# A decoder trunk on one core: the seventh product of a token-major step is issued inside the next channel-major step, and the first such step of each layer comes later

## The chip, the cores and the metric

The kernel runs on one core of a Trainium2 chip. The core has five engines with queues of their own: TensorE (PE in the profile; its weight loads are PEld), VectorE (DVE), ScalarE (ACT), GpSimd (POOL) and SyncE (SP), which issues the loads of weights. The metric is device time in microseconds of one execution. The kernel before has three runs: 2107.92, 2093.62 and 2107.99 us, median 2107.92.

## The reference

Two layers of a hybrid decoder on 256 tokens of width 2048, in float32. The core of a layer:

```python
h = rms_norm(x, norm1_g[l])
z = h @ w_in[l]                       # 2048 x 5120: q, k, v, gu, gv
mix = concatenate([attn(q, k, v), gmlp(gelu(gu), gelu(gv))])
x = x + mix @ w_out[l]                # 2048 x 2048
h2 = rms_norm(x, norm2_g[l])
x = x + square(relu(h2 @ w_up[l])) @ w_down[l]   # 2048 x 8192, 8192 x 2048
```

After both layers comes a last `rms_norm`. Nearly all of the work is the four weight products, and the two of the MLP (`w_up`, `w_down`) are about two thirds of it. The change is in the MLP.

## The kernel before, in words

**Numbers.** TensorE multiplies fp32r. To keep float32's accuracy each operand is split: `hi` is the value rounded to fp32r by a copy on ScalarE (L152, L170), `lo` the rest, by a subtraction on VectorE (L162, L175). A product is three matmuls: hi by hi, lo by hi, hi by lo. Activations are split in the same way; they lie in `hs` (the normalised input of a projection), `half` (1024 channels of an MLP's inner value) and `shared` (sums of pieces of `half`).

**Layout.** `x` stands transposed: 16 chunks of 128 channels by 256 tokens. A **channel-major step** (`transposed`, L352 to L385) takes a 512 x 256 piece of weights, with the weights stationary and 256 tokens moving: 2 column halves of 4 products, 24 matmuls of 128 x 256 into a bank `acc` (L380, L382, L384). A **token-major step** (`fast`, L387 to L413) has the activations stationary and 256 columns of weights moving. It computes a part of `w_down`'s first 512 columns with seven products of half-size blocks in place of eight, in the manner of Strassen and Winograd: seven products of 2 chunks of 3 matmuls, 42 matmuls (L408, L410, L411), which all accumulate in four banks `aux` that stay taken from a layer's first such step to its last. It needs four pieces: `Top`, `Bottom`, and two `Sums` of them that VectorE makes in place (L202 to L206). Of the activations, three of the seven products use `half` and four use `shared`, sums of blocks of `half` that VectorE makes (L729 to L732) and that are split in four parts (L611, L612).

**Order.** The MLP of a layer runs in nine rounds, `e` = 0 to 8. A round issues `w_up` for 1024 inner channels (16 steps; not in round 9), and `w_down` for the 1024 of the round before (not in round 1): 12 channel-major steps for columns 512 to 2047, and 2 token-major steps for columns 0 to 511. The token-major steps are put among the `w_up` steps (in round 9 among the `w_down` steps): behind the 4th and 8th of 16, and in round 9 behind the 3rd and 6th of 12. This list is written out (`steps`), and the program issues it step by step: ScalarE's `hi` and VectorE's `lo` are issued up to four steps ahead, loads as buffers come free (`load_more`). Other work (`later(delay, cost, fn)`) waits in a queue that is looked at once behind each step and spends a budget of 1.2 there; `soon` is for the same without a budget. The sums come by this queue behind a round's last `w_up` step, one part a step; `sums_ready()` issues what is still missing when a token-major step begins.

**A layer's end.** Behind the last token-major step `combine` (L741 to L753) reads the four banks and makes the four result blocks with seven additions on VectorE. Two `turn_back` (L755 to L761) transpose two blocks each on TensorE (four 128 x 128 transposes, L760), and `update` adds the result to `x` chunks 0, 1 and 2, 3 (L471, `x<-x,aux`). In layer 0 an update is followed by `hs` for the next layer (ScalarE L269, VectorE L273), a square (ScalarE L282) and the sum of squares (VectorE L286, `nacc`). In layer 1 the squares go to the last norm: a matmul with ones (L297), a square root (ScalarE L320), the spread of the factor (L305), the products with `x` (L877), and the stores.

In the program each engine executes its own instructions in the order in which they are issued.

Of the kernel before, what the change touches and what calls it, by code (L numbers as in the profile page):

```python
# [83 lines left out]
def trunk(ctx: ExitStack, tc: tile.TileContext, layout, xT, consts, gains, w, b_sp, w_sp, out):  # L84
# [37 lines left out]
    def acc_bank():  # L122
        return pacc.tile([P, 512], F32, name="acc", tag="acc")

    def aux_bank():
        return paux.tile([P, 512], F32, name="aux", tag="aux")
# [58 lines left out]
    class Bottom(Sub):  # L185


        left, right, frees = Top.left, Top.right, 0
# [23 lines left out]
    cols = cp.tile([P, (2 * DEPTH + 1) * KC + 2 * DEPTH * NH], F32, name="cols")  # L212
# [14 lines left out]
    def later(delay, cost, fn):  # L227

        queue.append((now[0] + delay, cost, fn))
# [107 lines left out]


    steps = []
    summed, sum_parts = [True], [None]  # L340

    def sums_ready():
        run_until(lambda: summed[0])

    def collect(fn, *args, **kw):
        n = len(steps)
        fn(*args, **kw)
        part = steps[n:]
        del steps[n:]
        return part  # L350

    def transposed(name, l, row0, nk, col0, ncols, moving, after, between=None, apart=False):  # L352

        order = [(c, k) for c in range(0, ncols, 256) for k in range(0, nk, 4)]
        if between:  # L360
            h = nk // 8
            order[h:2 * h], order[2 * h:3 * h] = order[2 * h:3 * h], order[h:2 * h]
        accs = {}
        for n, (c, k0) in enumerate(order):
            if between and n == nk // 4:
                mark(between)
            wt = Sub(name, l, row0 + k0 * P, col0 + c, 4, 256)

            def mm(wt=wt, k0=k0, c=c):
                two = apart and c == ncols - 256  # L370
                if k0 == 0:
                    accs[c] = [acc_bank(), acc_bank()] if two else acc_bank()
                ps = accs[c]
                for cb in range(2):
                    o = ps[cb][:, 0:S] if two else ps[:, cb * S:(cb + 1) * S]
                    for k in range(4):
                        xs = moving(k0 + k)
                        hi = wt.hi[:, k, cb * P:(cb + 1) * P]
                        last = k0 + k == nk - 1
                        pe.matmul(o, lhsT=hi, rhs=xs[:, 0, :], start=(k0 + k == 0 and (two or cb == 0)), stop=False,  # L380
                                  skip_group_check=True)
                        pe.matmul(o, lhsT=wt.lo[:, k, cb * P:(cb + 1) * P], rhs=xs[:, 0, :], start=False, stop=False,  # L382
                                  skip_group_check=True)
                        pe.matmul(o, lhsT=hi, rhs=xs[:, 1, :], start=False, stop=last, skip_group_check=True)  # L384
            steps.append((wt, mm, (lambda c=c: after(c, accs[c])) if k0 + 4 == nk else None))  # L385

    def fast(name, l, row0, col0, tiles, banks, first, last, done):  # L387

        for p in range(2):
            top, bottom = (cls(name, l, row0 + (4 * h + 2 * p) * P, col0, 2, 512) for h, cls in enumerate((Top, Bottom)))  # L390
            upper, lower = Sums(top, bottom, False), Sums(top, bottom, True)

            def mm(p=p, top=top, bottom=bottom, upper=upper, lower=lower):
                if first and p == 0:
                    banks.extend(aux_bank() for _ in range(4))
                half = tiles[0][0]
                sums_ready()
                extra = sum_parts[0]
                left, right = slice(0, 256), slice(256, 512)
                for n, (a, lower_rows, tt, b, cols) in enumerate((  # L400
                        (half, 0, 0, top, left), (half, 1, 0, bottom, left), (extra, 1, 0, bottom, right),
                        (extra, 1, 1, upper, left), (extra, 0, 1, upper, right),
                        (extra, 0, 0, lower, right), (half, 1, 1, lower, left))):
                    o = banks[n // 2][:, n % 2 * 256:n % 2 * 256 + 256]
                    for k in range(2):
                        xh, xl = (a[:, 4 * lower_rows + 2 * p + k, i, tt * P:(tt + 1) * P] for i in range(2))
                        hi, lo = b.hi[:, k, cols], b.lo[:, k, cols]
                        pe.matmul(o, lhsT=xh, rhs=hi, start=(first and p == 0 and k == 0 and n % 2 == 0), stop=False,  # L408
                                  skip_group_check=True)
                        pe.matmul(o, lhsT=xh, rhs=lo, start=False, stop=False, skip_group_check=True)  # L410
                        pe.matmul(o, lhsT=xl, rhs=hi, start=False, stop=(last and p == 1 and k == 1),  # L411
                                  skip_group_check=True)
            steps.append(((top, bottom, upper, lower), mm, done if p and last else None))  # L413

    def natural(name, l, col0, ncols, after):
# [20 lines left out]
    def mark(fn):  # L436

        steps.append((None, fn, None))
# [4 lines left out]
    def from_tiles(tiles, n):  # L443
        return lambda k: tiles[k // n][0][:, k % n, :, :]
# [21 lines left out]
    def update(norm, c, ps, final, last):  # L466

        alone = last and final and c == KC - 2
        for j in range(2) if alone else [slice(0, 2)]:
            xj = x[:, c + j, :] if alone else x[:, c:c + 2, :]  # L470
            vec.tensor_tensor(xj, xj, ps[j][:, 0:S] if alone else pair(ps)[:, j, :], op=OP.add)  # L471
        if final:
            if not last:
                norm.chunks(c)
            norm.square(c, alone)
            if last:
                norm.gain(c)

    def layer(l, n1, n2, n3, last):
# [261 lines left out]
        def combine():  # L741
            p1, p2, p3, p5, p7, p6, p4 = (banks[n // 2][:, n % 2 * 256:n % 2 * 256 + 256] for n in range(7))
            b1, u, c11, c12, c21, c22 = (blocks[:, n, :] for n in range(6))
            act.activation(b1, p1, AF.Copy)
            vec.tensor_tensor(u, b1, p6, op=OP.add)
            vec.tensor_tensor(c11, b1, p2, op=OP.add)
            vec.tensor_tensor(c22, u, p7, op=OP.add)
            vec.tensor_tensor(u, u, p5, op=OP.add)
            vec.tensor_tensor(c12, u, p3, op=OP.add)
            vec.tensor_tensor(c21, c22, p4, op=OP.subtract)  # L750
            vec.tensor_tensor(c22, c22, p5, op=OP.add)
            later(1, 1.5, lambda: turn_back(0, c11, c21))
            later(1, 1.5, lambda: turn_back(2, c12, c22))  # L753

        def turn_back(c, first, second):  # L755
            ps = aux_bank()
            for j in range(2):
                for tt, src in enumerate((first, second)):
                    o = j * S + tt * P
                    pe.transpose(ps[:, o:o + P], src[:, j * P:(j + 1) * P], ident)  # L760
            later(0, 1.5, lambda: update(n3, c, ps, True, last))  # L761
# [3 lines left out]
        for e in range(9):  # L765
            up, down, quick = [], [], []
            if e < 8:
                up = collect(transposed, "w_up", l, 0, KC, e * 1024, 1024, from_hs, after_up(e))
            if e:
                down = collect(transposed, "w_down", l, (e - 1) * 1024, 8, FAST, D - FAST, from_tiles([hid[e - 1]], NH),  # L770
                               lambda c, ps, e=e: update(n3, (c + FAST) // P, ps, e == 8, last), apart=last and e == 8)
                quick = collect(fast, "w_down", l, (e - 1) * 1024, 0, [hid[e - 1]], banks, e == 1, e == 8,
                                lambda: later(1, 1.5, combine))
            rest = up or down
            n = len(quick) + 1
            for i in range(n):
                steps.extend(rest[len(rest) * i // (n + 1):len(rest) * (i + 1) // (n + 1)] if quick else rest)
                steps.extend(quick[i:i + 1])
            if quick:
                steps.extend(rest[len(rest) * n // (n + 1):])  # L780
            if up:
                steps.extend(down)
        if last:
# [11 lines left out]
    for l in range(DEPTH):  # L795
        layer(l, norms[2 * l], norms[2 * l + 1], norms[2 * l + 2], l == DEPTH - 1)
# [74 lines left out]
    n = norms[-1]  # L871
# [43 lines left out]
```

## Time and profile before

| | |
|---|---|
| runs | 2107.92, 2093.62, 2107.99 us (median 2107.92) |
| profiled execution | 2093.35 us, span 2091.5 us, mean granted clock 0.994 |
| TensorE | 2066.8 us busy, 17066 matmul records |
| VectorE | 1464.4 us busy, 1800 instructions |
| ScalarE | 1008.9 us busy, 1265 instructions |
| HBM | 390.65 MB read, 188 GB/s over the span |

How to read it: times are microseconds from the span's start. A row of a timeline gives start, length, engine, line and operation with `out<-in`, and in brackets the idle time ahead of it with what ended it; neighbouring instructions of one kind are merged (`x2`). Matmuls are pipelined: a matmul of 256 columns is shown as about 280 ns long, but the next starts some 115 ns after it, so TensorE's busy share says that it had work, not how quickly it went through it. A row of a table of stretches gives the stretch, its length, TensorE's busy time with the count of matmuls, the granted clock, the share of the DMA engines and GB/s.

### The profile page before, as it was taken

What the parts mean: (1) busy time and instruction counts of PE and PEld (TensorE: products, weight loads), DVE (VectorE), ACT (ScalarE), POOL (GpSimd) and SP (SyncE); (2) the same over time, 40 slices, a digit from 0 to 9 for tenths busy, and PEclk for the clock granted to TensorE, in tenths of its full rate; (3) what the DMA queues carried; (4) which work ended last, traced back from release to release, by engine and by line L of the source; (5) the groups of instructions that cost most, each with busy time, mean ns of one, the idle gap of its engine ahead of it and who ended that gap; (6) DMA issues with size and microseconds to landing.
All of it is one profiled execution on the core that took longest, in us unless ns stands there. A gap on an engine that the chain in (4) does not pass through costs nothing. (4 is left out here: it accounts for less than half of the span.)

```text
span 2091.5 us, 40406 instructions
## 1 busy us (share of the span) xinstructions
PE 2066.8 (99%) x17066; PEld 2028.3 (97%) x17066; DVE 1464.4 (70%) x1800; ACT 1008.9 (48%) x1265; POOL 68.7 (3%) x90
## 2 busy tenths in 40 slices
PE   9999999999999999999999999999999999999997
PEld 8998999899999999999989999998999999999997
DVE  7666766777677677776856576667676676777666
ACT  7555454444454444544645554545353444444444
POOL 0002300000000000000000050000000000000000
PEclk9999999999999999999999999999999999999998
DMA  8555555365565655656565556555565655556543
GB/s 320 175 172 177 196 183 191 134 225 190 172 218 178 226 192 169 216 182 201 189 204 172 183 172 197 185 181 173 170 207 177 216 188 178 196 178 216 191 162 111
DMA packets 112118, 395.38 MB, mean 189 GB/s; under 512 B 12352, under 2 KB 16448, under 8 KB 111936
## 3 DMA queue, kind: packets, MB, share of 16 engines
q1 hardware_dynamic: 110800, 389.86, 55.6%
q8 instruction: 133, 2.18, 0.4%
q10 hardware_dynamic: 1136, 2.94, 0.4%
q14 instruction: 49, 0.40, 0.1%
HBM read 390.65 MB, written 2.10 MB: 188 GB/s over the span
## 5 line engine op out<-in xcount | busy, mean ns | idle before, releaser
L152 ACT ACTIVATE hi<-raw 128x1024 fp32r<-128x1024 f32 (+1 forms) x773 | 783.7, 1046 | 420.8 <-PE acc L384 194.5
L162 DVE TENSOR_TENSOR lo<-raw,hi 128x1024 fp32r<-128x1024 f32 (+1 forms) x773 | 907.8, 1211 | 42.0 <-ACT hi L152 25.8
L380 PE MATMUL acc<-hs,hi 128*128 128x256 f32 x2816 | 784.3, 279 | 0.0
L384 PE MATMUL acc<-hs,hi 128*128 128x256 f32 x2816 | 781.8, 278 | 0.0
L382 PE MATMUL acc<-hs,lo 128*128 128x256 f32 x2816 | 781.8, 278 | 0.0
L380 PE MATMUL acc<-half,hi 128*128 128x256 f32 x2048 | 569.5, 278 | 0.0
L382 PE MATMUL acc<-half,lo 128*128 128x256 f32 x2048 | 569.1, 278 | 0.0
L384 PE MATMUL acc<-half,hi 128*128 128x256 f32 x2048 | 569.0, 278 | 0.0
L380 PEld LDWEIGHTS acc<-hs,hi 128*128 128x128 f32 x2816 | 532.3, 189 | 0.4 <-issue 0.2
L382 PEld LDWEIGHTS acc<-hs,lo 128*128 128x128 f32 x2816 | 528.8, 188 | 0.4 <-issue 0.2
L384 PEld LDWEIGHTS acc<-hs,hi 128*128 128x128 f32 x2816 | 528.6, 188 | 0.0
L380 PEld LDWEIGHTS acc<-half,hi 128*128 128x128 f32 x2048 | 387.6, 189 | 0.0
L382 PEld LDWEIGHTS acc<-half,lo 128*128 128x128 f32 x2048 | 384.4, 188 | 0.1
L384 PEld LDWEIGHTS acc<-half,hi 128*128 128x128 f32 x2048 | 384.4, 188 | 0.0
L611 ACT ACTIVATE half<-ar 128x512 fp32r<-128x512 f32 x72 | 45.6, 633 | 323.5 <-DVE ar L716 308.9
L471 DVE TENSOR_TENSOR x<-x,acc 128x512 f32<-128x512 f32 (+1 forms) x113 | 76.7, 680 | 174.6 <-PE acc L384 174.6
L715 DVE TENSOR_TENSOR ar<-acc,nR 128x512 f32<-128x512 f32 x64 | 44.2, 691 | 196.0 <-PE acc L384 196.0
L431 PE MATMUL acc<-hi,hs 128*128 128x512 f32 x256 | 101.4, 396 | 0.5 <-ACT hs L269 0.5
L433 PE MATMUL acc<-hi,hs 128*128 128x512 f32 x256 | 100.8, 394 | 0.0
L432 PE MATMUL acc<-lo,hs 128*128 128x512 f32 x256 | 100.1, 391 | 0.0
L612 DVE TENSOR_TENSOR half<-ar,half 128x512 fp32r<-128x512 f32 x72 | 49.8, 692 | 50.3 <-ACT half L611 50.3
L408 PE MATMUL aux<-hi,shared 128*128 128x256 f32 x256 | 73.4, 287 | 10.4 <-ACT shared L611 10.4
(127 smaller groups left out, 1548.2 us busy)
## 6 DMA issues: line engine op xcount, KB each, us to landing
raw<-in_w SPq DMA_DIRECT2D x731, 512.0 KB, 4.5
raw<-in_w SPq DMA_DIRECT2D x10, 256.0 KB, 5.3
x<-in_xT SPq DMA_DIRECT2D x7, 256.0 KB, 5.6
out<-x SPq DMA_DIRECT2D x7, 256.0 KB, 3.1
shared<-in_b_sp ACTq DMA_DIRECT2D x2, 512.0 KB, 7.0
shared<-in_w_sp ACTq DMA_DIRECT2D x2, 512.0 KB, 8.5
con<-in_consts ACTq DMA_DIRECT2D x1, 512.0 KB, 7.4
x<-in_xT ACTq DMA_DIRECT2D x1, 256.0 KB, 4.2
```

The lines of the kernel that those rows point to most:

```text
L152: act.activation(self.h[:, j * m:(j + 1) * m], self.raw[:, j * m:(j + 1) * m], AF.Copy)
L162: vec.tensor_tensor(lo[:, r], self.raw[:, r], self.h[:, r].bitcast(F32), op=OP.subtract)
L380: pe.matmul(o, lhsT=hi, rhs=xs[:, 0, :], start=(k0 + k == 0 and (two or cb == 0)), stop=False, skip_group_check=True)
L382: pe.matmul(o, lhsT=wt.lo[:, k, cb * P:(cb + 1) * P], rhs=xs[:, 0, :], start=False, stop=False, skip_group_check=True)
L384: pe.matmul(o, lhsT=hi, rhs=xs[:, 1, :], start=False, stop=last, skip_group_check=True)
L408: pe.matmul(o, lhsT=xh, rhs=hi, start=(first and p == 0 and k == 0 and n % 2 == 0), stop=False, skip_group_check=True)
L431: pe.matmul(ps, lhsT=xh, rhs=hi, start=(k0 + k == 0), stop=False)
L432: pe.matmul(ps, lhsT=xh, rhs=lo, start=False, stop=False)
L433: pe.matmul(ps, lhsT=xl, rhs=hi, start=False, stop=(k0 + k == KC - 1))
L471: vec.tensor_tensor(xj, xj, ps[j][:, 0:S] if alone else pair(ps)[:, j, :], op=OP.add)
L611: act.activation(t[:, c:c + 2, 0, :], src, AF.Copy)
L612: vec.tensor_tensor(t[:, c:c + 2, 1, :], src, t[:, c:c + 2, 0, :].bitcast(F32), op=OP.subtract)
```

## The change

It has three parts. (1) A token-major step computes six of its products; the seventh is put into a list `held`, and the next channel-major step issues it behind its own first three matmuls. (2) The places of the token-major steps are given by step: in round 2, the first that has any, behind the 8th and the 12th `w_up` step (before: 4th and 8th), in rounds 3 to 8 behind the 4th and 8th (as before), in round 9 behind the 4th and 8th `w_down` step (before: 3rd and 6th). (3) `turn_back` is put off by two steps in place of one.

```diff
+    held = []
...
                     for k in range(4):
+                        if cb == 0 and k == 1 and held:
+                            held.pop()()
                         xs = moving(k0 + k)
...
-                for n, (a, lower_rows, tt, b, cols) in enumerate((
-                        (half, 0, 0, top, left), (half, 1, 0, bottom, left), (extra, 1, 0, bottom, right),
-                        (extra, 1, 1, upper, left), (extra, 0, 1, upper, right),
-                        (extra, 0, 0, lower, right), (half, 1, 1, lower, left))):
+
+                def product(n, a, lower_rows, tt, b, cols):
                     o = banks[n // 2][:, n % 2 * 256:n % 2 * 256 + 256]
                     for k in range(2):
...
+                for n, args in enumerate((
+                        (half, 0, 0, top, left), (half, 1, 0, bottom, left), (extra, 1, 0, bottom, right),
+                        (extra, 1, 1, upper, left), (extra, 0, 1, upper, right), (extra, 0, 0, lower, right))):
+                    product(n, *args)
+                held.append(lambda: product(6, half, 1, 1, lower, left))
...
-            later(1, 1.5, lambda: turn_back(0, c11, c21))
-            later(1, 1.5, lambda: turn_back(2, c12, c22))
+            later(2, 1.5, lambda: turn_back(0, c11, c21))
+            later(2, 1.5, lambda: turn_back(2, c12, c22))
...
-            n = len(quick) + 1
-            for i in range(n):
-                steps.extend(rest[len(rest) * i // (n + 1):len(rest) * (i + 1) // (n + 1)] if quick else rest)
-                steps.extend(quick[i:i + 1])
-            if quick:
-                steps.extend(rest[len(rest) * n // (n + 1):])
+            at = (8, 12) if e == 1 else (4, 8)
+            for i, one in enumerate(rest):
+                if quick and i in at:
+                    steps.append(quick.pop(0))
+                steps.append(one)
```

TensorE, end of a token-major step in round 2 or later, before: the sixth product's last matmul (`shared`), the seventh product (`half`, its three matmuls stand twice), and the channel-major step behind it.

```order
L411 MATMUL aux<-hi,shared 128x256
L408 MATMUL aux<-hi,half 128x256
L410 MATMUL aux<-lo,half 128x256
L411 MATMUL aux<-hi,half 128x256
L408 MATMUL aux<-hi,half 128x256
L410 MATMUL aux<-lo,half 128x256
L411 MATMUL aux<-hi,half 128x256
L380 MATMUL acc<-hs,hi 128x256
L382 MATMUL acc<-hs,lo 128x256
L384 MATMUL acc<-hs,hi 128x256
```

The same place of the changed kernel, whose lines are numbered some higher:

```order
L414 MATMUL aux<-hi,shared 128x256
L383 MATMUL acc<-hs,hi 128x256
L385 MATMUL acc<-hs,lo 128x256
L387 MATMUL acc<-hs,hi 128x256
L411 MATMUL aux<-hi,half 128x256
L413 MATMUL aux<-lo,half 128x256
L414 MATMUL aux<-hi,half 128x256
L411 MATMUL aux<-hi,half 128x256
L413 MATMUL aux<-lo,half 128x256
L414 MATMUL aux<-hi,half 128x256
L383 MATMUL acc<-hs,hi 128x256
```

The seventh product's six matmuls moved behind three matmuls of the channel-major step, which goes on behind them.

ScalarE in round 2 of layer 0, before, from the last `w_up` product of round 1 (`half`, the first row): `hi` of 128 x 512 is the first token-major step's `Top`, the next three `hi` belong to it too (`Bottom` and the two `Sums`), and the four `shared` are the parts of the sums.

```order
L611 ACTIVATE half<-ar 128x2x256
L152 ACTIVATE hi<-raw 128x1024 x2
L611 ACTIVATE shared<-ar 128x2x256
L152 ACTIVATE hi<-raw 128x1024
L611 ACTIVATE shared<-ar 128x2x256
L152 ACTIVATE hi<-raw 128x1024
L611 ACTIVATE half<-ar 128x2x256
L611 ACTIVATE shared<-ar 128x2x256
L152 ACTIVATE hi<-raw 128x1024
L611 ACTIVATE shared<-ar 128x2x256
L152 ACTIVATE hi<-raw 128x1024 x2
L170 ACTIVATE hi<-raw 128x512
```

The same place in the changed kernel, from the same row:

```order
L620 ACTIVATE half<-ar 128x2x256
L152 ACTIVATE hi<-raw 128x1024 x2
L620 ACTIVATE shared<-ar 128x2x256
L152 ACTIVATE hi<-raw 128x1024
L620 ACTIVATE shared<-ar 128x2x256
L170 ACTIVATE hi<-raw 128x512
L620 ACTIVATE half<-ar 128x2x256
L620 ACTIVATE shared<-ar 128x2x256
L152 ACTIVATE hi<-raw 128x1024
L620 ACTIVATE shared<-ar 128x2x256
L152 ACTIVATE hi<-raw 128x1024 x3
L620 ACTIVATE half<-ar 128x2x256
```

Before, the first step's `Top` stood ahead of the first of these rows, and the `hi` of 128 x 512 at the end is the second token-major step's; now the one between the second and third `shared` is the first step's, and all four `shared` are issued while channel-major steps are still to come.

VectorE at the end of layer 0, before, from the last `lo` ahead of an update (names with buffer numbers): `x<-x,acc` adds a channel-major block to `x`, `x<-x,aux` a block that came by `turn_back`.

```order
L162 TENSOR_TENSOR lo_11816<-raw_11694,hi_11778 128x1024
L471 TENSOR_TENSOR x_82<-x_82,acc_11784 128x512
L273 SCALAR_TENSOR_TENSOR hs_83<-x_82,cols_80,hs_83 128x256 x2
L286 TENSOR_TENSOR nacc_11424<-nacc_11424,nsq_11849 128x512
L471 TENSOR_TENSOR x_82<-x_82,aux_11773 128x512
L273 SCALAR_TENSOR_TENSOR hs_83<-x_82,cols_80,hs_83 128x256 x2
L286 TENSOR_TENSOR nacc_11424<-nacc_11424,nsq_11857 128x512
L162 TENSOR_TENSOR lo_11862<-raw_11696,hi_11814 128x1024
L471 TENSOR_TENSOR x_82<-x_82,aux_11809 128x512
```

And in the changed kernel:

```order
L162 TENSOR_TENSOR lo_11880<-raw_11757,hi_11842 128x1024
L480 TENSOR_TENSOR x_82<-x_82,acc_11848 128x512
L273 SCALAR_TENSOR_TENSOR hs_83<-x_82,cols_80,hs_83 128x256 x2
L286 TENSOR_TENSOR nacc_11422<-nacc_11422,nsq_11913 128x512
L480 TENSOR_TENSOR x_82<-x_82,aux_11873 128x512
L273 SCALAR_TENSOR_TENSOR hs_83<-x_82,cols_80,hs_83 128x256 x2
L286 TENSOR_TENSOR nacc_11422<-nacc_11422,nsq_11930 128x512
L162 TENSOR_TENSOR lo_11935<-raw_11759,hi_11878 128x1024
L480 TENSOR_TENSOR x_82<-x_82,aux_11916 128x512
```

The rows read alike, but the `x<-x,acc` among them is before the one of step 10 of round 9's twelve, with the last block's to follow behind both `x<-x,aux`; in the changed kernel it is the last block's, and behind it stand only the two `x<-x,aux`. In layer 1 the last block's update, in two halves of 128 x 256, stood behind both `x<-x,aux` and now stands ahead of them.

## The prediction

> **What bounds the kernel now.** I read the page first, then TensorE's waits, then busy time by stretches, because a TensorE that is always busy can still run at two speeds. In the fence: the page's head and first part, and TensorE's waits (line waited for: us in all, times, longest).
>
> ```profile
> span 2091.5 us, 40406 instructions
> ...
> PE 2066.8 (99%) x17066; PEld 2028.3 (97%) x17066; DVE 1464.4 (70%) x1800; ACT 1008.9 (48%) x1265; POOL 68.7 (3%) x90
> ...
> PE aux L408 <- ACT shared L611: 10.4, 2, 5.2
> PE aux L305 <- DVE nr L331: 1.2, 1, 1.2
> PE aux L760 <- DVE ar L750: 1.1, 1, 1.1
> ```
>
> TensorE sets the time: 99% busy, and the only long waits are two of 5.2 us, one a layer, in a token-major step (L408) for the last piece of `shared`. The execution took 2093.35 us, its span 2091.5; 1.85 us lie around it. The runs are 2107.92, 2093.62 and 2107.99: the profiled execution is like the lowest, 14.6 us under the median.
>
> Now the stretches of layer 0's third round (first three rows: first token-major step, the four channel-major steps behind it, second token-major step; fourth: the next four channel-major steps), then of longer ones. The count in brackets is a little above the program's, since ends of older matmuls reach in.
>
> ```profile
> 482.92:487.68 4.76, 4.76 (x44) 1.00 0.09 34
> 487.68:498.99 11.31, 11.31 (x98) 1.00 0.70 234
> 498.99:503.94 4.95, 4.95 (x44) 1.00 0.30 105
> 503.94:514.83 10.89, 10.89 (x98) 1.00 0.89 329
> 832.93:849.20 16.27, 16.27 (x141) 1.00 0.57 194
> 1445.21:1518.00 72.79, 72.79 (x620) 1.00 0.56 188
> 1887.44:1960.23 72.79, 72.79 (x620) 1.00 0.55 188
> 2058.79:2065.02 6.23, 6.23 (x54) 1.00 0.00 0
> ```
>
> Four channel-major steps are 96 matmuls (24 each). They take 10.89 us in one place and 11.31 in another, at a granted clock of 1.00 in both: 113.4 ns and 117.8 ns from matmul to matmul, the short pace and the long one, 4.4 ns apart. DMA does not choose between them: its share is 0.89 at the short pace and 0.70 at the long. The place does. The first token-major step keeps the short pace that it found (4.76 us for 42 matmuls, 113.3 ns), and behind it the pace is long; the second keeps the long pace (4.95, 117.9), and behind it the pace is short. So entering a token-major step changes nothing, and leaving one for a channel-major step, a **seam**, turns the pace over, in both directions. In layer 0 the long pace lasts from first to second token-major step (16.27 us, row five, in each of seven rounds; the ninth round's is a step shorter). In layer 1 the phase is the other one, and it lasts from the second to the next round's first (72.79 us, six times, first and sixth quoted), and from the last seam to the transposes (6.23 us).
>
> Where layer 1's phase comes from shows in layer 0 and layer 1's first token-major steps (as above; the third row is the part after layer 1's wait) and in the matmul that waited:
>
> ```profile
> 388.21:401.37 13.16, 7.97 (x44) 0.74 0.48 154
> 1417.02:1429.55 12.53, 7.33 (x44) 0.73 0.45 140
> 1423.72:1428.16 4.44, 4.42 (x19) 0.50 0.38 117
> 1423.72 0.58 PE L408 MATMUL aux<-hi,shared 128*128 128x256 f32 x1 [5.18 <-ACT shared L611]
> ```
>
> Both steps have the wait, then some 4.4 us at half the granted clock. Behind layer 0's the pace is long, behind layer 1's short. Which phase a layer gets seems to be drawn there.
>
> **The sum, part by part.** *Seams.* In before each token-major step has one seam. In after it is 36 matmuls, 3 of the next channel-major step, 6 held ones, the other 21: two seams. If each turns the pace, the second undoes the first, and only 9 matmuls a step go at the other pace. Long now: layer 0, seven times 4x24+42 and once 3x24+42, 1080 matmuls; layer 1, six times 24x24+42, once 23x24+42, and 48, 4350. At 4.4 ns that is 4.8 and 19.1 us. (The difference, 14.3, is the difference of the runs, 2107.92 less 2093.62: as if layer 0 had got layer 1's phase there.) The last round's part, 114 and 90 matmuls, 0.9 us, is inside the two sums on the layers' ends below; so **-23.0**. New: 32 steps x 9 x 4.4 ns = **+1.3**.
>
> *The wait.* Layer 0's first token-major step took 13.16 us, layer 1's 12.53, each 4.76 without wait and half clock: 8.4 + 7.8, **-16.2**. It goes only if the data are there four steps later; VectorE around it in before:
>
> ```profile
> 377.53 0.69 DVE L715 TENSOR_TENSOR ar<-acc,nR 128x512 f32<-128x512 f32 x1 [3.53 <-PE acc L384]
> ...
> 397.31 1.22 DVE L162 TENSOR_TENSOR lo<-raw,hi 128x1024 fp32r<-128x1024 f32 x1
> ```
>
> From the former round's last product (377.53) to 397.31 VectorE had made the sums, their four parts, and all `lo` of the step. In after three more `lo` stand among them (of the steps now ahead), 1.15 each: 400.8. The step starts at 388.21 + 4x2.72 = 399.1 and wants its last `lo` 30 matmuls later, 402.5. So 1.7 us to spare, and nothing new waits; bounds 0 and the full 16.2.
>
> *Layer 0's end.* Round 9 has its token-major steps behind the 4th and 8th of 12 steps, not the 3rd and 6th, so the blocks are combined later, and the next layer's first step needs `x` chunks 0 and 1, which they make. VectorE's updates, ScalarE's `hs`, and TensorE's first token-major step and next layer in before:
>
> ```profile
> 998.08 0.28 PE L408 MATMUL aux<-hi,half 128*128 128x256 f32 x1
> ...
> 1002.37 0.68 DVE L175 TENSOR_TENSOR lo<-raw,hi 128x512 fp32r<-128x512 f32 x1
> ...
> 1005.87 0.69 DVE L471 TENSOR_TENSOR x<-x,acc 128x512 f32<-128x512 f32 x1 [0.22 <-PE acc L384]
> ...
> 1032.55 0.68 DVE L471 TENSOR_TENSOR x<-x,aux 128x512 f32<-128x512 f32 x1
> ...
> 1035.34 1.22 DVE L162 TENSOR_TENSOR lo<-raw,hi 128x1024 fp32r<-128x1024 f32 x1
> 1036.48 0.68 DVE L471 TENSOR_TENSOR x<-x,aux 128x512 f32<-128x512 f32 x1
> ...
> 1033.27 0.91 ACT L269 ACTIVATE hs<-x,cols 128x256 fp32r<-128x256 f32 x2 [1.36 <-DVE x L471]
> ...
> 1035.00 0.39 PE L431 MATMUL acc<-hi,hs 128*128 128x512 f32 x1
> 1037.75 0.51 PE L431 MATMUL acc<-hi,hs 128*128 128x512 f32 x1
> ```
>
> VectorE, not TensorE, sets this end: from 1005.87 it waits for TensorE no more, and `x<-x,aux` starts 26.68 us later. In after the same rows follow in the same order, up to `x<-x,aux`, behind the update of step 6. Count from the start S of the first token-major step. The update of step 4 starts at S and lasts 2.79 (1032.55 to 1035.34), four `lo` take 4x1.15, and 1002.37 to the end of the next `lo` is 3.28: S+10.7 (TensorE is there at S+10.5). Then 26.68, and 1.17 to ScalarE's first half: the next layer's first matmul at S+38.55. TensorE is through at S+32.3 (276 matmuls, two groups of transposes) and waits 6.3 us. S itself is a step, 2.72, later than 998.08: 41.3 against 36.92. The next layer's second step needs the second `x<-x,aux`, 3.93 later, at 45.2 against 39.67 (1037.75): +5.5. After waits of 5.2 the clock was half for 4.4 us (0.50 above); then the 12 matmuls of 2.75 us take some 5.0, the second wait is swallowed, and the second step starts at 46.3: **+6.6**, which I take. Bounds: +2.0 if VectorE had caught up (last update and `x<-x,aux` still follow the last matmul, 3.96 us), +7.9 if half clock lasts 1.2 longer. The 1.1 us wait of the transposes, gone with the delay of 2, is inside.
>
> The Trainium skill, "TensorE: Matmul & The Clock Gate", section "What's actually happening", says the clock halves after an idle window of about 3.4 us, free-running. The 0.50 row agrees; by that rule a 6.3 us wait is always punished, without it the term would be 5.5.
>
> *The kernel's end*, likewise (first token-major step; the accumulated squares; the square root):
>
> ```profile
> 2040.90 0.28 PE L408 MATMUL aux<-hi,half 128*128 128x256 f32 x1
> ...
> 2073.21 0.68 DVE L471 TENSOR_TENSOR x<-x,aux 128x512 f32<-128x512 f32 x1
> 2074.59 0.69 DVE L286 TENSOR_TENSOR nacc<-nacc,nsq 128x512 f32<-128x512 f32 x1 [0.70 <-ACT nsq L282]
> 2075.20 0.68 DVE L471 TENSOR_TENSOR x<-x,aux 128x512 f32<-128x512 f32 x1
> ...
> 2077.33 1.05 PE L297 MATMUL aux<-ones,nacc 128*128 128x1 f32 x8 [0.71 <-DVE nacc L286]
> ...
> 2079.31 0.26 ACT L320 ACTIVATE nr<-aux,warm 128x2 f32<-128x2 f32 x1
> ```
>
> Now the last block's update comes last; in after both `x<-x,aux` follow it. TensorE ends at S+32.1, the last update takes 0.7, the two rounds of update, square and sum 1.99 each (2073.21 to 2075.20), ScalarE's gain of the last block, which stands ahead of the first square, 0.6, and 2.0 go to the square root (2077.33 to 2079.31): S+39.4, with the 2.72 that S is later 42.1 against 38.41: **+3.7**, between +3.1 without the 0.6 and +4.7 with another round of ScalarE in the way.
>
> *At nothing:* `lower`'s buffers are held 9 matmuls, 1.0 us, longer, covered by the four steps that ScalarE and VectorE work ahead; without that cover up to 1.0 us per step, 32 in all. No row of SyncE or GpSimd moves; the same loads are issued in the same number.
>
> Sum: 2093.35 - 23.0 + 1.3 - 16.2 + 6.6 + 3.7 = 2065.8, **2066 us**: 27 under its own execution, 42 under the median.
>
> **Rivals.** (1) *One turn a step.* What turns the pace is the end of a whole token-major step, or three matmuls are too few. Then both layers, entered at the short pace, look like layer 0 now: 2x4.8 long, less the part in the ends (2x0.5), without the 1.3: 2073. For it: no row shows two seams so close. Against: each of the seams now turns it, whatever came before.
> (2) *The wait stays in small, and decides the phase: slower.* If VectorE's 1.7 us at the first token-major step are not there, TensorE waits there and leaves at the long pace; with paired seams nothing turns it back, and the whole layer stays long. From that step to the end of the ninth round are some 5400 matmuls; without the hundred at its end that VectorE covers that is 23 us a layer at 4.4 ns: one layer 2089, both 2112, slower than both the median and the profiled execution. It decides from the first wait long enough to upset the pace; the two known cases waited 5.2 us and left once each way. Against: short pace at that place in both layers, and the 1.7.
> (3) *The pace does not follow the order*: it goes on as now, and only the wait is won: 2093.35 - 16.2 + 6.6 + 3.7 = 2087. [...] The rows contradict that: 113.4 and 117.8, sorted by place. Hence few chances.
>
> **How the numbers follow.** Forecast 0.64; rival 1, 0.13; rival 2, one layer 0.05 and both 0.10; rival 3, 0.05; otherwise, such as longer ends, 0.03. Terms known only by bounds move the forecast from 2060 (ends +2.0 and +3.1) to 2070. The range holds forecast, rival 1, rival 3 and one long layer: 2059 to 2089. More than 1% under the median is under 2086.8 (1% is about what a measurement of this kernel tells from no change): forecast, rival 1 and half of "otherwise", 0.79. Within 1%: rival 3 and rival 2, 0.19. Slower by more, over 2129, would need both layers long and longer ends: 0.02.
>
> **What would show it.** Right: no wait of L408's successor for `shared`; channel-major steps of 2.72 us throughout both layers, with 72.79 shrunk to 70.1; a TensorE wait near 6 us, with half clock, at layer 1's first step; the square root some 7.5 us after the last channel-major matmul, not 3. Wrong: 16 us stretches at 117.8 ns (rival 1), a whole layer of them (rival 2), 72.79 again (rival 3). The forecast fails most easily in the ends, where VectorE may be less or more behind than I count.

## The result and the profile after

The changed kernel takes 2112.1 us (median of 20 runs, 2091.13 to 2113.56), the kernel before in the same comparison 2093.67 (20 runs, 2077.70 to 2107.99). The ratio is 1.0068, 95% interval 1.0040 to 1.0096: a little slower. The forecast was 2066; the result is the time of rival 2 with both layers long, 2112.

The single runs say more than the medians. Before has three clusters: three runs at 2077.7 to 2079.0, twelve between 2092.1 and 2094.5, five between 2107.3 and 2108.0. They are some 14 to 15 us apart, where the prediction worked out 14.3 for one layer that goes from one phase to the other. After has sixteen runs between 2110.7 and 2113.6, three at 2091.1 to 2092.4, and one at 2107.4. So the changed kernel does not always lose the same; no trace here shows one of its four shorter runs.

The profiled execution of the changed kernel took 2111.68 us. The fence shows the head and first part of its page, then TensorE's waits (line waited for: us in all, times, longest). In the changed kernel's numbering a channel-major step's three matmuls are L383, L385 and L387, a token-major step's L411, L413 and L414.

```profile
span 2109.9 us, 40413 instructions
...
PE 2086.4 (99%) x17066; PEld 2048.5 (97%) x17066; DVE 1465.6 (69%) x1800; ACT 1009.5 (48%) x1265; POOL 68.7 (3%) x90
...
PE acc L440 <- ACT hs L269: 5.0, 2, 4.3
PE aux L297 <- DVE nacc L286: 4.6, 1, 4.6
PE acc L385 <- DVE lo L162: 1.9, 3, 1.1
```

The two waits of 5.2 us for `shared` are gone, as the change's second part promises. New are the waits at the layers' ends (L440, 4.3 us, and L297), which were forecast, and three short ones for a `lo` at L385, 1.9 us in all, which were not. The other 0.7 us of L440 lie at the kernel's start. TensorE is busy for 19.6 us more than before with the same number of matmuls, so they ran at a longer pace. By stretches: four channel-major steps behind the first and behind the second token-major step of round 2, in layer 0 and in layer 1, then the 24 steps between the second token-major step of round 3 and the first of round 4, all less the three matmuls ahead of the held product:

```profile
405.20:415.76 10.56, 10.56 (x95) 1.00 0.72 241
420.97:431.93 10.96, 10.96 (x96) 1.00 0.95 345
1450.15:1460.70 10.55, 10.55 (x96) 1.00 0.70 240
1465.94:1476.90 10.96, 10.96 (x96) 1.00 0.95 352
1543.63:1611.12 67.49, 67.49 (x575) 1.00 0.60 202
```

The program has 93 matmuls in each of the first four rows: 113.5 ns each behind the first token-major step, 117.8 behind the second, in both layers. In the last row it is 573, and 67.49 us are 117.8 ns again. From the second token-major step of round 2 layer 1 is long to its end, and layer 0 until round 9. So one place in each layer decided; here are TensorE's rows at layer 0's, the last matmul of the token-major step, the three matmuls, the first held one, and the channel-major step going on:

```profile
419.73 0.28 PE L414 MATMUL aux<-hi,shared 128*128 128x256 f32 x1
419.84 0.28 PE L383 MATMUL acc<-hs,hi 128*128 128x256 f32 x1
419.96 0.38 PE L385 MATMUL acc<-hs,lo 128*128 128x256 f32 x1
420.18 0.28 PE L387 MATMUL acc<-hs,hi 128*128 128x256 f32 x1
420.29 0.28 PE L411 MATMUL aux<-hi,half 128*128 128x256 f32 x1
...
420.97 0.28 PE L383 MATMUL acc<-hs,hi 128*128 128x256 f32 x1
421.09 0.28 PE L385 MATMUL acc<-hs,lo 128*128 128x256 f32 x1
```

Between the second and the third of the three matmuls lie 0.22 us instead of 0.11 or 0.12; the matmul that reads `lo` (L385) is shown 0.38 us long, not 0.28. That is a wait of 0.1 us, too short to be listed. Behind it the six held matmuls go at the short pace (420.29 to 420.97, 113 ns each), and behind the second seam the pace is long. VectorE before and at that place, then two rows of TensorE's weight loads there:

```profile
415.96 0.69 DVE L724 TENSOR_TENSOR ar<-acc,nR 128x512 f32<-128x512 f32 x1 [1.37 <-PE acc L387]
416.69 0.69 DVE L725 SCALAR_TENSOR_TENSOR ar<-ar 128x512 f32<-128x512 f32 x1
418.08 0.69 DVE L621 TENSOR_TENSOR half<-ar,half 128x512 fp32r<-128x512 f32 x1 [0.70 <-ACT half L620]
418.69 3.49 DVE L162 TENSOR_TENSOR lo<-raw,hi 128x1024 fp32r<-128x1024 f32 x3
```

```profile
419.73 0.19 PEld L383 LDWEIGHTS acc<-hs,hi 128*128 128x128 f32 x1
419.95 0.19 PEld L385 LDWEIGHTS acc<-hs,lo 128*128 128x128 f32 x1
```

The token-major step stands where a block of `w_up` has just been finished. VectorE makes that block's part of `half` first (L724, L725, a wait for ScalarE, L621: 2.73 us from 415.96 to 418.69) and only then the `lo` of the channel-major step that takes the held product. The first of these three is 1.22 us long, as such a row is in the prediction's fence (397.31), so it is done at 419.91. TensorE loads that `lo` as a weight, and the loads around it are 0.11 to 0.12 us apart: it was due at 419.84 or 419.85 and came at 419.95, just behind the end of the `lo`. Before, that `lo` was wanted six matmuls, some 0.7 us, later, behind all 42 of the token-major step. At the first token-major step of the round the same `lo` is later still:

```profile
403.48 0.28 PE L383 MATMUL acc<-hs,hi 128*128 128x256 f32 x1
404.16 0.39 PE L385 MATMUL acc<-hs,lo 128*128 128x256 f32 x1 [0.39 <-DVE lo L162]
```

The gap is 0.68 us where it should be 0.11, and this one the phase survived, in layer 1 as well (a gap of 0.67 at 1448.43). At layer 1's second token-major step the wait is again 0.1 us (1464.90 to 1465.12), but there the held matmuls went at the long pace, as they should behind one seam, and it was the second seam that did not turn it back. In layer 0's ninth round waits at the same kind of place did both: at the first token-major step two gaps of 0.20 and 0.22 us (1015.40 to 1015.82) left the pace short for the next 93 matmuls,

```profile
1016.65:1027.20 10.55, 10.55 (x96) 1.00 0.58 197
```

and at the second a wait of 1.1 us (1032.68, the longest of the three at L385) left it long again.

### The profile page after: what moved, and what is told of

Its sections match the earlier page's. It is cut to its first block, busy times and chain, and to the rows that moved or that the text cites. A ratio compares the mean times of both kernels' runs of the same rounds, so it can differ in the third digit from the quotient of the medians.

```text
span 2109.9 us, 40413 instructions
## 1 busy us (share of the span) xinstructions
PE 2086.4 (99%) x17066; PEld 2048.5 (97%) x17066; DVE 1465.6 (69%) x1800; ACT 1009.5 (48%) x1265; POOL 68.7 (3%) x90
## 4 chain that ended last, share of the span: by engine, by line
PE 96%; DVE 2%; ACT 1%; issue 1%; DMA 0%; ACTq 0%; DVEq 0%
PE acc L385 26%; PE acc L383 26%; PE acc L387 26%; PE acc L440 3%; PE acc L442 3%; PE acc L441 3%; PE aux L411 2%; PE aux L414 2%; PE aux L413 2%; DVE lo L162 1%; PE aux L666 0%; PE aux L610 0%; PE aux L568 0%; PE aux L297 0%; PE aux L597 0%
## 5 line engine op out<-in xcount | busy, mean ns | idle before, releaser
L383 PE MATMUL acc<-hs,hi 128*128 128x256 f32 x2816 | 787.9, 280 | 0.0
L385 PE MATMUL acc<-hs,lo 128*128 128x256 f32 x2816 | 785.8, 279 | 0.8 <-DVE lo L162 0.8
L387 PE MATMUL acc<-hs,hi 128*128 128x256 f32 x2816 | 785.4, 279 | 0.0
L385 PE MATMUL acc<-half,lo 128*128 128x256 f32 x2048 | 573.0, 280 | 1.1 <-DVE lo L162 1.1
L383 PE MATMUL acc<-half,hi 128*128 128x256 f32 x2048 | 573.1, 280 | 0.0
L387 PE MATMUL acc<-half,hi 128*128 128x256 f32 x2048 | 572.8, 280 | 0.0
L383 PEld LDWEIGHTS acc<-hs,hi 128*128 128x128 f32 x2816 | 535.3, 190 | 0.4 <-issue 0.2
L385 PEld LDWEIGHTS acc<-hs,lo 128*128 128x128 f32 x2816 | 528.7, 188 | 1.6 <-DVE lo L162 1.2
L387 PEld LDWEIGHTS acc<-hs,hi 128*128 128x128 f32 x2816 | 528.6, 188 | 0.0
L383 PEld LDWEIGHTS acc<-half,hi 128*128 128x128 f32 x2048 | 390.8, 191 | 0.0
L385 PEld LDWEIGHTS acc<-half,lo 128*128 128x128 f32 x2048 | 384.5, 188 | 1.4 <-DVE lo L162 1.3
L387 PEld LDWEIGHTS acc<-half,hi 128*128 128x128 f32 x2048 | 384.4, 188 | 0.0
L724 DVE TENSOR_TENSOR ar<-acc,nR 128x512 f32<-128x512 f32 x64 | 44.2, 691 | 193.6 <-PE acc L387 193.6
L440 PE MATMUL acc<-hi,hs 128*128 128x512 f32 x256 | 102.5, 401 | 5.0 <-ACT hs L269 5.0
L621 DVE TENSOR_TENSOR half<-ar,half 128x512 fp32r<-128x512 f32 x72 | 49.9, 693 | 50.3 <-ACT half L620 50.3
L269 ACT ACTIVATE hs<-x,cols 128x256 fp32r<-128x256 f32 x64 | 29.0, 501 | 90.4 <-DVE x L480 89.0
```

What stands on the lines that cost most here:

```text
L440: pe.matmul(ps, lhsT=xh, rhs=hi, start=(k0 + k == 0), stop=False)
L621: vec.tensor_tensor(t[:, c:c + 2, 1, :], src, t[:, c:c + 2, 0, :].bitcast(F32), op=OP.subtract)
L724: vec.tensor_tensor(z, pair(ps), n2.R[:, None, :].to_broadcast([P, 2, S]), op=OP.mult)
```

## The experiments

The theory after these rows: each seam turns the pace; two seams close together undo each other; and the late `lo` puts a short wait of TensorE inside the pair, which leaves the pace turned. Up to round 9 nothing turns it back later: at the long pace TensorE wants the `lo` later by 37 times 4.4 ns, 0.16 us, and no longer waits for it, so a long layer stays long, while a short one is exposed at every token-major step. Where the expectations use letters, A is this theory; the others are its rivals, each with its numbers. The kernel before took 2093.17 us (median of 11 runs) beside the first four experiments and 2092.87 (median of 7) beside the last four.

### The `lo` of the step that takes the held product, one step earlier

```diff
-            low_to(done + 1 + ahead)
+            low_to(done + 1 + ahead + (n + 1 < len(steps) and isinstance(steps[n + 1][0], tuple)))
```

VectorE gets this `lo` ahead of the block's L724; nothing else in the program is changed.

> The changed kernel, but in the step ahead of a token-major step VectorE makes one more `lo`, that of the channel-major step which takes the held product; so this `lo` stands ahead of the 2.7 us of work on the finished w_up block, not behind it. Theory A: two seams leave the pace as it was, and the layers are long because this `lo` comes about 0.1 us too late for the three matmuls, which want it 6 matmuls sooner than before; the short wait upsets the phase. Then TensorE waits nowhere at a seam, both layers keep the short pace to their end (2.72 us a channel-major step), and the time falls by two layers of some 23 us, from 2112 to about 2066. Rival B: two seams so close do not give the short pace back, whatever waits: both layers stay long, 2110 to 2112.

2068.35 us (four runs, 2067.54 to 2068.88), ratio to before 0.9894 (0.9858 to 0.9930): 43.8 us under the changed kernel. VectorE has the third `lo` now ahead of L724 (first two rows), and TensorE goes through the place without a gap (next five). Then, from the stretches, layer 0's two of 93 matmuls, and layer 1's 573:

```profile
412.40 3.66 DVE L162 TENSOR_TENSOR lo<-raw,hi 128x1024 fp32r<-128x1024 f32 x3
415.97 0.69 DVE L724 TENSOR_TENSOR ar<-acc,nR 128x512 f32<-128x512 f32 x1
...
419.18 0.28 PE L383 MATMUL acc<-hs,hi 128*128 128x256 f32 x1
419.30 0.28 PE L385 MATMUL acc<-hs,lo 128*128 128x256 f32 x1
419.42 0.28 PE L387 MATMUL acc<-hs,hi 128*128 128x256 f32 x1
419.54 0.28 PE L411 MATMUL aux<-hi,half 128*128 128x256 f32 x1
...
420.25 0.28 PE L383 MATMUL acc<-hs,hi 128*128 128x256 f32 x1
...
404.55:415.10 10.55, 10.55 (x95) 1.00 0.56 187
420.25:430.80 10.55, 10.55 (x95) 1.00 0.86 299
1520.31:1585.26 64.95, 64.95 (x575) 1.00 0.60 200
```

From 419.18 to 420.25 the nine matmuls go at some 119 ns, then 113.4 again (10.55 / 93, 64.95 / 573). So the pair does what it was forecast to do, and the late `lo` alone kept it from doing so. Against the changed kernel, which reaches layer 0's first token-major step at the same 399.40, the trace gains 19.8 us up to layer 1's first token-major step (1424.54 against 1444.35) and 23.1 from there to the end.

This trace also has the bare effect once, in layer 0's ninth round, between the first and second matmul of a channel-major step, 21 matmuls behind the last seam:

```profile
1012.25 0.28 PE L387 MATMUL acc<-half,hi 128*128 128x256 f32 x1
1012.36 0.28 PE L383 MATMUL acc<-half,hi 128*128 128x256 f32 x1
1012.68 0.39 PE L385 MATMUL acc<-half,lo 128*128 128x256 f32 x1
1012.90 0.28 PE L387 MATMUL acc<-half,hi 128*128 128x256 f32 x1
1013.02 0.28 PE L383 MATMUL acc<-half,hi 128*128 128x256 f32 x1
```

A gap of 0.32 us, a wait of 0.2. Ahead of it the matmuls are 113.8 ns apart, behind it 117.8 (from 1013.02 for the rest of the layer's channel-major steps).

### The places and the delay, without the held product

```diff
-                held.append(lambda: product(6, half, 1, 1, lower, left))
+                product(6, half, 1, 1, lower, left)
```

> The changed kernel, but the seventh product is computed in the token-major step itself, so there is one seam a step and the first three matmuls of the next step are wanted 6 matmuls later. Theory A: no 5.2 us wait, so both layers enter the first token-major step at the short pace; each seam turns it, and the long pace lasts 16.3 us in each round from first to second token-major step in both layers: 2066 - 1.3 + 2x4.8, some 2074. Rival C, the phase is drawn by chance whether there is a wait or not, or the new places themselves make the layers long: 72.8 us stretches in one layer or both, 2088 or 2103.

2075.63 us (eight runs, 2074.80 to 2076.72), ratio 0.9903 (0.9865 to 0.9941). The stretches from first to second token-major step of round 3, in layer 0 and layer 1:

```profile
480.01:496.27 16.26, 16.26 (x141) 1.00 0.58 194
1507.65:1523.91 16.26, 16.26 (x140) 1.00 0.57 195
```

Each is 138 matmuls at 117.8 ns. So it is in every round from the second on, and between the second token-major step and the next round's first the pace is short: single seams turn the pace, and without the wait for `shared` both layers get the cheaper phase. These two parts of the change are worth 17.5 us against the median of before.

### The held product, with the old places and delay

```diff
-            later(2, 1.5, lambda: turn_back(0, c11, c21))
-            later(2, 1.5, lambda: turn_back(2, c12, c22))
+            later(1, 1.5, lambda: turn_back(0, c11, c21))
+            later(1, 1.5, lambda: turn_back(2, c12, c22))
...
-            at = (8, 12) if e == 1 else (4, 8)
+            at = (3, 6) if e == 8 else (4, 8)
```

> The held product alone: places of the token-major steps and the delay of 1 as before the change. Theory A: the 5.2 us waits stay, and behind them each layer is at one pace all through, since its seams come in pairs, unless the late `lo` upsets it: with both layers long some 2069 + 46 = 2115, with one long 2092. If the late places are what costs (rival C), this one is not above 2094 and shows no long layer.

2095.58 us (one run). The waits of 5.2 us are there again (L411 for `shared`: 10.4 us, twice). One layer is long, the other short, in the two rows of 40 us from the middle of each, so a long layer needs no late places (rival C):

```profile
600.00:640.00 40.00, 40.00 (x342) 1.00 0.63 223
1600.00:1640.00 40.00, 40.00 (x353) 1.00 0.47 162
```

Layer 0 fell at its second token-major step, with a gap of 219 ns (416.91 to 417.13). Layer 1 came through thirteen pairs with gaps of 220 ns (the first at 1464.31) and stayed short. In the changed kernel gaps of 218 and 221 ns at this place did turn it (419.96 and 1464.90). So a wait of 0.1 us does not turn the pace every time, and its size does not tell the cases apart. What does, stays open.

### The round 9 of before, with the earlier `lo`

```diff
-            at = (8, 12) if e == 1 else (4, 8)
+            at = (8, 12) if e == 1 else (3, 6) if e == 8 else (4, 8)
```

(against the first experiment's kernel)

> The kernel with the earlier `lo`, and round 9's token-major steps back behind the 3rd and 6th step. Theory A: the waits at the layers' ends go (in the changed kernel 5.0 us at layer 1's first step with half clock behind it, and 4.6 us ahead of the last squares' sum): about 8 to 10 us less than with the earlier `lo` alone, 2056 to 2058. If the ends were hidden anyway: 2066, the same.

2064.41 us (four runs, 2064.12 to 2064.76), ratio 0.9875 (0.9840 to 0.9911): 3.9 us under the first experiment, not the 10 that the forecast's ends would give back, nor nothing. The waits fell only in part. The first two rows are the first experiment's (1.1 of its 7.8 us lie at the kernel's start, 6.7 at layer 0's end), the last two this one's:

```profile
PE acc L440 <- ACT hs L269: 7.8, 2, 6.7
PE aux L297 <- DVE nacc L286: 4.5, 1, 4.5
```

```profile
PE acc L440 <- ACT hs L269: 5.6, 2, 3.6
PE aux L297 <- DVE nacc L286: 3.0, 1, 3.0
```

The 5.0 us of the expectation hold 0.7 from the kernel's start, too; layer 0's end had 4.3. In before the same places cost no such waits. There, TensorE stood still for two times 5.2 us and ran at the long pace for part of the time, and the `turn_back` came one step sooner. The held product alone has the old places and delay, and its layer 1 was short throughout; yet it waited only 0.7 us for the last squares (L297), so the long pace is not needed for that. Which of the others made room for VectorE stays open.

### A foreign matmul in place of the held product

```diff
+                held.append(lambda: pe.matmul(acc_bank()[:, 0:1], lhsT=ones, rhs=ones[:, 0:1], start=True, stop=True))
```

(against the second experiment's kernel: all seven products stay in the token-major step, and one float32 matmul of a single column goes behind the next three; its result is not used)

> The new places with one seam a step (the seventh product in the token-major step), and behind the next channel-major step's first three matmuls one float32 matmul of 128x1 into a spare bank, whose result nobody uses. In the traces so far the pace behind float32 matmuls (transposes, column sums) is always the short one. Theory A with that: each seam turns the pace, the small matmul sets it to short again, no stretch of 16.3 us at the long pace is left; 9.6 us are won and 32 small matmuls of some 0.25 us paid, about 2074. Rival: a foreign matmul has no effect on the pace, or turns it like a seam: the 16.3 us stretches stay or wander, 2083 or more.

2076.07 us (one run). The long stretches of 16.26 us are gone and the pace is short throughout, but the small matmul costs about what that wins. So it need not be the held product: another matmul at that place can bring the short pace back too. The expectation's ground, that the pace behind float32 matmuls is always short, was too wide: behind a layer's first transposes it was 118.0 ns in the changed kernel (1042.21 and 2086.12, 24 matmuls each).

### Three seams in place of two

```diff
-                        if cb == 0 and k == 1 and held:
-                            held.pop()()
+                        if cb == 0 and k in (1, 2) and held:
+                            held.pop(0)()
...
-                        (extra, 1, 1, upper, left), (extra, 0, 1, upper, right), (extra, 0, 0, lower, right))):
+                        (extra, 1, 1, upper, left), (extra, 0, 1, upper, right))):
...
+                held.append(lambda: product(5, extra, 0, 0, lower, right))
```

(against the first experiment's kernel: the sixth product is held too, one product goes behind three matmuls and one behind six)

> The kernel with the earlier `lo`, but two products are held, the sixth behind three and the seventh behind six matmuls of the next channel-major step: three seams a step. Theory A counts seams: an odd number turns the pace, so the stretches from first to second token-major step of each round are long in both layers, 9.6 us, and 6 more matmuls a step go at the other pace, 2068 + 10 = 2078. Rival D, it is not the number but that channel-major matmuls stand between the products: all short as with two seams, 2068.

2077.0 us (one run). Three seams turn the pace as one does; first to second token-major step, layer 0 and layer 1:

```profile
480.46:496.70 16.24, 16.24 (x141) 1.00 0.59 197
1509.19:1525.43 16.24, 16.24 (x140) 1.00 0.63 197
```

With the held product in place and no late `lo`, the number of seams, odd or even, gives the pace.

### The held product behind 15 matmuls

```diff
-                        if cb == 0 and k == 1 and held:
+                        if cb == 1 and k == 1 and held:
```

(against the first experiment's kernel)

> The kernel with the earlier `lo`, the seventh product held behind 15 matmuls, not 3. Theory A: two seams, so both layers stay short; 12 more matmuls a step run at the long pace, 32 x 12 x 4.4 ns = 1.7 us: 2070. If the two seams have to lie close to undo each other: long stretches as with one seam a step, 2078, or long layers, 2112.

2069.96 us (one run), 1.6 above the first experiment. The 15 matmuls between the seams are long, the three channel-major steps behind them short:

```profile
478.10:479.87 1.77, 1.77 (x17) 1.00 0.27 42
480.58:488.74 8.16, 8.16 (x74) 1.00 0.62 204
```

1.77 us for 15 are 118 ns, 8.16 for 72 are 113.3. Twelve matmuls more at 4.4 ns, 32 times, are 1.7 us. The rows show the price of the stretch between two seams; the total agrees, but it is one run, and the first experiment's four spread over 1.3 us.

### Round 9's token-major steps as early as they go

```diff
-            at = (8, 12) if e == 1 else (3, 6) if e == 8 else (4, 8)
+            at = (8, 12) if e == 1 else (2, 5) if e == 8 else (4, 8)
```

(against the kernel of the fourth experiment)

> The kernel with the earlier `lo`, round 9's token-major steps behind the 2nd and 5th step. If the end of a layer is set by how late the blocks are combined, a step sooner wins up to 2.7 us at each end, and no more than the 5.6 and 3.0 us that TensorE still waits there: 2060 to 2062. If VectorE's amount of work in round 9 sets it, the same as behind the 3rd and 6th: 2064.

2054.32 us (four runs, 2053.79 to 2054.44), ratio 0.9792 (0.9741 to 0.9843): 38.6 us under before and 57.8 under the changed kernel. It is 10.1 under the fourth experiment, where 2.7 at each end was the most expected: at layer 0's end the waits fell from 5.6 us to 0.8, by more than the step is long, which that bound had excluded. Why, no run shows.

```profile
PE acc L440 <- ACT hs L269: 1.1, 2, 0.8
PE aux L297 <- DVE nacc L286: 0.7, 1, 0.7
```

At layer 0's end the half clock is gone with the wait: the granted clock is 1.00 in the 9.8 us behind it (1025.16 to 1035.00), and its mean over the span is 0.997, against 0.993 in the first experiment. Of the 14.0 us between the two kernels, 10.5 are the waits (7.8 + 4.5 less 1.1 + 0.7, the kernel's start included); of the rest some 3.0 are what 6.08 us at half clock cost there.

## Why the prediction was wrong

**The step that failed is "The wait".** It is right in what it removed: the waits for `shared` are gone. It fails at "So 1.7 us to spare, and nothing new waits". The margin was worked out for one datum, the token-major step's own last `lo`; that one was in time (VectorE had it done at 400.25, just ahead of L724, and it was wanted 30 matmuls behind 399.40, at 402.8). But the edit moves a second deadline: the three matmuls ahead of the held product want the next channel-major step's `lo` six matmuls sooner than before, and that `lo` stands on VectorE behind the block that ended with the step before. The row for it was in the profile of before, behind the block that ended at the second token-major step:

```profile
415.60 5.76 DVE L162 TENSOR_TENSOR lo<-raw,hi 128x1024 fp32r<-128x1024 f32 x5
```

Its first `lo` is done at 416.82 (1.22 us long), and TensorE loaded it (L382) at 417.63: 0.8 us to spare. Six matmuls sooner takes 0.71 of that, and the 36 matmuls ahead, at the short pace that the change was to bring, 0.16 more; nothing is left, where the prediction counted 1.7. It did not ask what the moved matmuls read. The wait is 0.1 us at the place that mattered. The first experiment changes only this and gives back 43.8 us.

**Rival 2 named the mechanism and the price**, not the place. It put the wait at the first token-major step, for its own data; there the phase survived a wait of 0.56. "From that step to the end of the ninth round" 23 us a layer was right: 23.1 measured in layer 1. In layer 0 19.8 are left; a long layer gives VectorE more time, and the wait at its end shrinks (4.3 against 6.7 us), with the half clock behind it (3.2 against 6.1 us). That rival 2's 2112 was met to 0.1 us is partly luck: the ends cost 2.9 us more than forecast, and layer 0 lost 3.3 us less than 23.1. The chance, 0.10 for both layers, rested on the margin of the one datum that was looked at.

**"Seams" held, where no wait falls into the pair.** Pairs undo each other (first experiment), odd numbers turn (second and sixth), the direction of the pace does not matter, and the stretch between costs 4.4 ns a matmul (seventh). With the `lo` in time the kernel lands at 2068.35, where the forecast had 2066.

**The ends were sized too small.** "Layer 0's end +6.6" measures +8.3: from the first token-major step of round 9 to layer 1's first token-major step the first experiment takes 435.42 us and before 418.94; 10.88 of that are the four steps by which layer 1's was put later, and 2.72 more come in because S is itself one step later: 435.42 + 2.72 - 418.94 - 10.88 = 8.3. The wait is 6.70 us (6.3 forecast); what was undersized is the half clock behind it, counted as 4.4 us:

```profile
1028.89 0.80 PE L440 MATMUL acc<-hi,hs 128*128 128x512 f32 x1 [6.70 <-ACT hs L269]
...
1028.89:1034.97 6.08, 6.08 (x14) 0.50 0.73 280
```

It lasted 6.08 us. The profile of before already had a figure near it: the prediction's "some 4.4 us at half the granted clock" behind both waits holds for layer 1's only. Behind layer 0's it was

```profile
394.91:400.75 5.84, 5.83 (x25) 0.50 0.46 137
```

"The kernel's end +3.7" measures +4.9 (52.74 + 2.72 from the same step to the end of the span, against 50.60). Forecast plus these two misses, 2065.8 + 1.7 + 1.2 = 2068.7; the first experiment's profiled execution took 2068.8. The Trainium skill, "TensorE: Matmul & The Clock Gate", section "What's actually happening", has the clock halve after an idle window of about 3.4 us; at layer 0's end the waits of 6.70 us (first experiment), 4.3 (changed kernel) and 3.6 (fourth) were followed by half clock, and behind the 0.8 us of the last experiment none shows, so the traces agree. The prediction's "always punished" at 6.3 us goes further than the rule: a free-running window fits whole into every wait only from twice its length, an estimate of 6.8 us from that figure.

**"At nothing"** was right for `lower`: no row shows a wait for it. Rival 1 (three matmuls are too few) is excluded by the first experiment. Rival 3, a pace that does not follow the order, falls with every table of stretches here.

## What to carry to other kernels

When instructions are moved ahead, list every datum that the moved ones *and the ones that now come sooner* read, and look up on the producing engine what stands in front of it; a margin for one datum is none for the next. A busy share of 99% hides the pace: divide stretches by the number of matmuls, and let clusters among the runs of one kernel tell how many phases there are and what each is worth. If a fast phase can be lost to a wait of 0.1 us and then stays lost for hundreds of matmuls, give its data a whole step of room: with it the runs of the best kernel lie within 0.7 us, where those of before spread over 30.

## What the runs showed of the hardware

The same stream of 128 x 256 matmuls with their weight loads has two steady paces, 113.4 and 117.8 ns at a granted clock of 1.00, and keeps the one it has over more than 570 matmuls. Leaving the token-major kind for the channel-major kind turns it over, entering does not; one float32 matmul of one column behind three others went with the short pace at all 32 places; a wait of 0.2 us among channel-major steps turned short to long once. Of waits near 0.1 us some turned it (gaps of 218, 219 and 221 ns) and some did not (220, thirteen times), and two of 0.55 and 0.56 us within a pair did not. A wait turned it the other way too, from long to short (gaps of 0.20 and 0.22 us at 1015.40 in the changed kernel). The half clock behind waits of 3.6 to 6.7 us lasted between 3.1 and 6.1 us. Why there are two paces, and what state carries them, no run here shows.
